# Six adaLN units computed in pairs, with their weights in an early pool and in idle buffers

## The chip, the cores and the metric

The kernel runs on one core of one Trainium2 chip. The metric is the device time of one execution in microseconds (us); lower is better.

## The reference

Two request groups go through one hybrid layer with the same weights: a prompt of 1024 frames and a sample of 32 frames. Everything is float32. Each group has its own conditioning vector `c`.

```python
mod = jax.nn.silu(c) @ w_ada + b_ada                 # 1024 -> 6 * 1024
sh1, sc1, g1, sh2, sc2, g2 = jnp.split(mod[:, None, :], 6, axis=-1)
h = x * (1 + sc1) + sh1
mq, mk, mv, mo, mi, mf, fq, fk, fv, ff, gu, gv = jnp.split(h @ w_in, split_at, axis=-1)
hm = mLSTM(mq, mk, mv, mo, mi, mf)                   # 4 heads, chunk-recurrent matrix memory
hf = forgetting_attention(fq, fk, fv, ff)            # 8 heads, causal softmax with a decay
hg = gu * spatial_gate(layer_norm(gv))               # gMLP
mix = jnp.concatenate([hm, hf, hg], -1) @ w_o
x = layer_norm(ALPHA * x + (1 + g1) * mix)
h = x * (1 + sc2) + sh2
y = (silu(h @ w_gate) * (h @ w_up)) @ w_down
x = layer_norm(ALPHA * x + (1 + g2) * y)
```

The first line, the adaLN product, is what the change touches. It is a product of a 1024 x 6144 matrix with two vectors, so nearly all of its cost lies in bringing 25 MB of weights to the core and in feeding TensorE a moving operand 256 columns wide for a result of two rows.

## The kernel before

**Numbers.** Every large product is done as three matmuls on float32 values split into a high and a low part (`hi*hi`, `hi*lo`, `lo*hi`), in three consecutive lines of the helpers (L130 to L132 in `gemm`, L402 to L404 in `tm_unit`).

**AdaLN units.** The 6144 columns are cut into 24 units of 256 columns; one unit is 1024 x 256 weights, 1 MB, loaded as two halves of 512 KB (`ada_load`). Units 0 to 7 hold shift and scale of the first modulation, 8 to 15 those of the second, 16 to 19 the gate `g1`, 20 to 23 the gate `g2`. `ada_parts(units, raws, ...)` computes one unit or a pair of units. For each half of each unit it makes four matmuls (L202); the trace shows each as two, so 16 rows a unit. They land in four strips of 32 partitions of one PSUM bank. ScalarE copies the bank to SBUF (L206, tile `adas`), TensorE transposes the two halves of the copy (L211, two instructions), VectorE sums the strips (L213) and adds the bias (`ada_end`, L219 and L223). One bank, one copy, one pair of transposes and one sum serve a whole group, be it one unit or two. The results go to the tile `mod`.

**Stages in order of time.** `fm_first` (to about 58 us) computes units 0 to 7 one by one between the first projection's products. Then two value units follow: `tm_unit(w1[0])` and `tm_unit(w1[1])`, each with one sample tile and eight tiles of 128 frames. A tile takes 24 matmuls of 264 columns, its PSUM bank is one of three (pool `pg`), and `evac_v` empties it: ScalarE copies the bank to `traw` (L434, two buffers), SyncE's queue stores `traw` to the output `o_v`, VectorE splits it into `vhl` (two buffers) and the queue stores that to the scratch tensor `dv`. Between tile 0 and tile 1 of the second value unit stands the pair of units 16 and 17 (`group`), whose four halves lie in the pool `pe`, tag `early`, with `EB` buffers. `tie` keeps the pair's matmuls behind the last matmul of the tile.

After that the constant `ORDER` is read word by word: `q` is a head's projection, `f` a head's attention for the first four blocks, `g` the next part of the gates (`gates`), `S` and `s` the decay of the sample and the start of the mLSTM states, `k` a key unit, `v`, `o` and `G` further projections, `m` an mLSTM chunk, and each `a` one adaLN unit from the list `rest` (`more(1)`). `T1[3]` units are taken ahead of the second part of the gates. So before the change the list is 18, 19, 8 to 15: units 18 and 19 are computed one by one at the gates, the others one at each of the eight `a`. All ten use the pool `pl`, tag `late`, with two buffers, which hold one unit. The pairs 20, 21 and 22, 23 come later, in the stage after the first layer norm.

**What sets the order.** The program is written in this order, but the tile framework's planner (`schedule_with_timeline_sim=True`) puts the instructions of each engine into a queue of its own. It takes an instruction when, by its reckoning, its inputs and its buffer are ready, and takes the one that was written first if several are. `high_priority(HPA)` moves `f` and `m` forward by 200. The queues are fixed when the program is built: on the chip each engine runs its queue in order, and waits at an instruction until its semaphores allow it. Nearly all loads and stores are in one queue, that of SyncE (SP). A pool opened in the space of a closed one can use a buffer only when the tiles that lay there are done with (`reuse_waits="tile"`).

**Buffers named by the change.** `mx` is at this point the pool `mx0`, opened when `pe` is closed. Its tags `mqk` (two buffers), `mb` and `mw` (one each) are used by the gates, by the decay of the sample and by every mLSTM chunk; `k1`, `k2`, `qp`, `q2` (two each) hold the operands of the heads in turn.

Of the kernel before, what the change touches and what calls it, by code (L numbers as in the profile page):

```python
# [7 lines left out]
F32 = mybir.dt.float32  # L8
F32R = mybir.dt.float32r
# [6 lines left out]
P = 128  # L16
D = 1024
KT = 8
S = 1024
# [13 lines left out]
LWE = 1  # L33
NB = (3, 2, 2)
PRE = 5
EB = 4
T1 = (0, 0, 0, 2)
XB, AB = (3, 6)
HPA = 200
MLB = (1, 2, 3, 4, 5)  # L40
RESE = "pp"
TAFF = ("aaaaaaaa", "aaaaaaav")
ORDER = "q0 f0 g q1 a f1 a g S q2 f2 k1p s a q3 f3 a v q4 f4 a q5 f5 o a m0 G0 q6 f6 a m1 G1p G2p q7 m2 f7 a m3 G3"
FP = (0, 0)
RAW = 3
WAKE = (10, 11)
# [19 lines left out]
def f(ap):  # L66
    return ap.bitcast(F32)


class Kernel:  # L70
# [115 lines left out]
    def ada_load(self, u, pool, tag, bufs):  # L186
# [3 lines left out]
            self.load(raws[half], self.d["w_ada"][u, :, half * 1024:(half + 1) * 1024])  # L190
        return raws

    def ada_parts(self, units, raws, ppool, ptag):
        self.phase = "ada"
        nc = self.nc
        n = len(units)
        ps = self.t(ppool, [P, 512], F32, ptag)
        steps = [(i, half) for half in ((0, 1) if units[0] < 8 else (1, 0)) for i in range(n)[::1 if half else -1]]
        for step in steps:
            i, half = step  # L200
            for k in range(4):
                nc.tensor.matmul(ps[32 * k:32 * k + 32, :256], self.c32[:, 4 * half + k, 6 - 2 * i:38 - 2 * i],  # L202
                                 raws[i][half][:, k * 256:(k + 1) * 256], start=step == steps[0],
                                 stop=step == steps[-1])
        a = self.t(self.pada, [P, 256], F32, "adas", 2)
        nc.scalar.copy(a, ps[:, :256])  # L206
        yield
        self.phase = "ada"
        pt = ps[:, 256:512]
        for half in range(2):  # L210
            nc.tensor.transpose(pt[:, half * P:(half + 1) * P], a[:, half * P:(half + 1) * P], self.ident)  # L211
        m = self.t(self.pada, [P, 2, 8], F32, "adam", 2)[:, :, :2 * n]
        nc.vector.tensor_reduce(m, pt.rearrange("p (h g j) -> p h j g", h=2, g=4)[:, :, 0:2 * n, :], AX.X, ALU.add)  # L213
        for i, u in enumerate(units):
            self.ada_end(u, m[:, :, 2 * i:2 * i + 2])
# [1283 lines left out]
    def run(self):  # L1499
        nc, tc, d = self.nc, self.tc, self.d  # L1500
        dr = self.pool("dr", space=DRAM)
        t = lambda shape, tag: self.t(dr, shape, F32, tag)
# [50 lines left out]
        sl = ExitStack()  # L1553
        self.pl = self.pada = self.pool("pl", ctx=sl)
        w1 = d["w_in_v"]
        rest = [18, 19] + list(range(8, 16))

        def more(n):
            for u in rest[:n]:
                self.ada((u,), self.pl, "late", 2, self.pt, "t")  # L1560
            del rest[:n]

        more(T1[0])
        se = ExitStack()
        pe = self.pool("pe", ctx=se, side="right")

        def group(units):
            def go():
                first = len(nc.cur_bb.bb.instructions)
                target = self.lastmm  # L1570
                for _ in self.ada_parts(units, raws, self.pt, "t"):
                    pass
                self.tie(nc.cur_bb.bb.instructions[first:], target, (mybir.EngineType.PE,))
                self.phase = "tm"
            raws = [self.ada_load(u, pe, "early", EB) for u in units]
            return go

        self.tm_unit(w1[0], 264, self.evac_v(0))
        self.tm_unit(w1[1], 264, self.evac_v(1), between={0: group((16, 17))})
        se.close()  # L1580
        s2 = ExitStack()
        self.mx = self.pool("mx0", ctx=s2)
        more(T1[2])
        gates = self.gates()
        next(gates)
        more(T1[3])
        self.foxbufs = (2, 2, 2, 2, 3)
        self.heads = {}

        def emit(x):  # L1590
            eng = nc.gpsimd if x[-1] == "p" else nc.vector
            x = x.rstrip("p")
            i = int(x[1:] or 0)
            if x[0] == "g":
                next(gates, None)
                return ()
            if x[0] == "f":
                return self.fox(i, ((0, 1, 2, 3),))
            if x[0] == "m":
                return self.mlstm(i)  # L1600
            if x[0] == "q":
                self.head_unit(i)
            elif x[0] == "k":
                self.fm_unit(w3[0], self.evac_mqk(3, 0.125), eng=eng)
            elif x[0] == "S":
                self.sample_decay()
            elif x[0] == "G":
                self.tm_unit(w2[2 + i % 2], 256, (self.evac_gv, self.evac_gmlp)[i % 2],
                             range(4 * (i // 2), 4 + i // 2 * 5), eng=eng)
            elif x[0] == "s":  # L1610
                self.mlstm_states()
            elif x[0] == "a":
                more(1)
            else:
                self.tm_unit(w2["vo".index(x)], 256, self.evac_raw((self.dmv, self.dmo)["vo".index(x)]), eng=eng)
            return ()

        for x in ORDER.split():
            if x[0] in "fm" and HPA:
                with tc.high_priority(HPA):  # L1620
                    weave(*[iter(emit(y)) for y in x.split("+")])
            else:
                weave(*[iter(emit(y)) for y in x.split("+")])
# [112 lines left out]
        t = self.t(self.pz, [P, 4, n], F32R, "z0", 1)  # L1736
# [129 lines left out]
```

## Time and profile before

| | |
|---|---|
| median of 3 runs | 1346.33 us (1344.91 to 1347.18) |
| profiled execution | 1346.69 us, span of its instructions 1344.9 us |
| TensorE (PE) busy | 1324.0 us, 98% |
| VectorE (DVE), ScalarE (ACT), GpSimd (POOL) busy | 989.1, 655.8, 231.9 us |
| granted TensorE clock | 0.998 |
| DMA | 221.73 MB, mean 165 GB/s |

How to read it: the span runs from the first to the last instruction; the execution's own time holds 1.8 us more. PE is the matmul stream, PEld the weight loads that overlap it; a busy PE is not one at its peak, since matmuls are pipelined and their ends are modelled. In a timeline a row gives the start, the length, the engine, the line, the operation, the tiles written and read, the number of merged instructions and, in brackets, the idle time before it with what ended it. `SPq` is SyncE's DMA queue: the row is the issue, not the transfer.

### The profile page before, as it was taken

The numbers are of one execution on the slowest core, as the hardware profiler recorded it, in microseconds if no ns is written. First come the engines' busy times: TensorE is split into PE (matmuls) and PEld (weight loads), VectorE is DVE, ScalarE is ACT, GpSimd is POOL, SyncE is SP. The second block draws the span as 40 slices with busy tenths as digits, with TensorE's granted clock in tenths as the row PEclk, the third lists the DMA queues.
The fourth block names the chain that finished last, engine by engine and source line by source line (L and its number), as shares of the span: only waits on it lengthen the run. The fifth ranks groups of instructions, "written<-read, shape, count | busy, mean of one in ns | idle before, by whom it ended". The sixth has DMA issues, their size and how long they took to land.

```text
span 1344.9 us, 25607 instructions
## 1 busy us (share of the span) xinstructions
PE 1324.0 (98%) x9684; PEld 1208.3 (90%) x9684; DVE 989.1 (74%) x2091; ACT 655.8 (49%) x1305; POOL 231.9 (17%) x263
## 2 busy tenths in 40 slices
PE   9999999999999999999999999999999999999996
PEld 6798888888999888888888888999999999999995
DVE  5635655678779667686876776678979887988777
ACT  3413445455547545545454454435754453635355
POOL 0102100143246100000000001464610000000341
PEclk9999999999999999999999999999999999999999
DMA  9585465546557754454344332663785858554221
GB/s 362 207 299 154 150 204 186 174 131 207 181 195 257 191 136 130 117 163 126 115 121 116 110 104 82 217 175 112 205 231 154 228 148 225 139 175 131 89 79 67
DMA packets 119450, 221.73 MB, mean 165 GB/s; under 512 B 18580, under 2 KB 62768, under 8 KB 119328
## 3 DMA queue, kind: packets, MB, share of 16 engines
q1 hardware_dynamic: 112096, 207.55, 49.0%
q0 software_dynamic: 6032, 11.94, 5.2%
q8 instruction: 76, 1.25, 0.4%
q10 hardware_dynamic: 1200, 0.62, 0.2%
q14 instruction: 46, 0.38, 0.1%
HBM read 188.13 MB, written 51.85 MB: 178 GB/s over the span
## 4 chain that ended last, share of the span: by engine, by line
PE 68%; DVE 4%; DMA 1%; ACT 1%; issue 1%; DVEq 0%; ACTq 0%
PE up_g L130 6%; PE up_g L132 6%; PE up_g L131 6%; PE dn_g L130 4%; PE dn_g L132 4%; PE dn_g L131 4%; PE sup_u L132 3%; PE sup_u L131 3%; PE sup_u L130 3%; PE wo_g L131 2%; PE wo_g L132 2%; PE wo_g L130 2%; PE sup_g L132 2%; PE sup_g L131 2%; PE sup_g L130 2%; PE fox_t L943 2%
## 5 line engine op out<-in xcount | busy, mean ns | idle before, releaser
L130 PE MATMUL up_g<-tm_ah,up_whi 128*128 128x512 f32 (+1 forms) x384 | 140.0, 365 | 0.0
L131 PE MATMUL up_g<-tm_al,up_whi 128*128 128x512 f32 (+1 forms) x384 | 140.0, 365 | 0.0
L132 PE MATMUL up_g<-tm_ah,up_wlo 128*128 128x512 f32 (+1 forms) x384 | 139.7, 364 | 0.0
L1368 ACT CAST sup_whi<-sup_raw 128x1024 fp32r<-128x1024 f32 x54 | 56.1, 1048 | 89.3 <-PE dn_u L131 43.9
L130 PEld LDWEIGHTS up_g<-tm_ah,up_whi 128*128 128x128 f32 x384 | 72.3, 188 | 11.1 <-DVE tm_al L1246 0.4
L132 PEld LDWEIGHTS up_g<-tm_ah,up_wlo 128*128 128x128 f32 x384 | 72.3, 188 | 11.1
L131 PEld LDWEIGHTS up_g<-tm_al,up_whi 128*128 128x128 f32 x384 | 72.3, 188 | 10.7
L916 ACT ACTIVATE fox_p<-fox_s,fox_fmx 128x384 f32<-128x384 f32 (+2 forms) x96 | 55.2, 579 | 53.0 <-DVE fox_fmx L914 41.2
L1199 DVE SCALAR_TENSOR_TENSOR wo_z<-dn_g,start_mod,wo_z 128x512 f32<-128x512 f32 (+4 forms) x120 | 60.3, 521 | 22.6 <-PE dn_g L132 22.0
L118 DVE TENSOR_TENSOR up_wlo<-up_raw,up_whi 128x1024 fp32r<-128x1024 f32 x50 | 65.2, 1305 | 15.0 <-ACT up_whi L117 13.7
L1369 DVE TENSOR_TENSOR sup_wlo<-sup_raw,sup_whi 128x1024 fp32r<-128x1024 f32 x54 | 68.0, 1263 | 10.7 <-ACT sup_whi L1368 10.7
L117 ACT CAST up_whi<-up_raw 128x1024 fp32r<-128x1024 f32 x50 | 52.4, 1048 | 47.2 <-PE up_g L131 23.9
L130 PE MATMUL dn_g<-up_acth,dn_whi 128*128 128x512 f32 (+2 forms) x200 | 73.5, 368 | 0.8 <-DVE wo_z L1199 0.8
L132 PE MATMUL dn_g<-up_acth,dn_wlo 128*128 128x512 f32 (+2 forms) x200 | 73.3, 366 | 0.0
L131 PE MATMUL dn_g<-up_actl,dn_whi 128*128 128x512 f32 (+2 forms) x200 | 72.8, 365 | 0.0
L948 ACT CAST fox_pth<-fox_t 128x512 fp32r<-128x512 f32 (+1 forms) x80 | 41.6, 542 | 59.2 <-PE fox_t L943 57.5
L117 ACT CAST dn_whi<-dn_raw 128x1024 fp32r<-128x1024 f32 (+1 forms) x44 | 42.7, 971 | 51.7 <-PE up_g L131 16.0
L911 DVE TENSOR_REDUCE fox_fmx<-fox_s 128x1 f32<-128x384 f32 (+2 forms) x96 | 52.8, 553 | 16.3 <-PE fox_s L908 15.0
L949 DVE TENSOR_TENSOR fox_ptl<-fox_t,fox_pth 128x512 fp32r<-128x512 f32 (+1 forms) x80 | 49.9, 631 | 15.9 <-ACT fox_pth L948 15.6
L118 DVE TENSOR_TENSOR dn_wlo<-dn_raw,dn_whi 128x1024 fp32r<-128x1024 f32 (+1 forms) x44 | 49.5, 1125 | 10.4 <-ACT dn_whi L117 9.5
L402 PE MATMUL tm_g<-tm_whi,start_h1h 128*128 128x256 f32 (+1 forms) x192 | 55.3, 288 | 0.7 <-DVE tm_traw L477 0.7
L1320 POOL DMA_DIRECT2D start_dp<-w_gu x19 | 19.8, 1067 | 209.0 <-DMA start_dp<-w_gu 209.0
(684 smaller groups left out, 4799.7 us busy)
## 6 DMA issues: line engine op xcount, KB each, us to landing
up_raw<-w_gu SPq DMA_DIRECT2D x50, 512.0 KB
ada_late<-w_ada SPq DMA_DIRECT2D x28, 512.0 KB
dn_raw<-w_dn SPq DMA_DIRECT2D x28, 512.0 KB
sup_raw<-w_gu SPq DMA_DIRECT2D x20, 512.0 KB
start_dp<-w_gu SPq DMA_DIRECT2D x19, 512.0 KB
start_dp<-w_gu POOLq DMA_DIRECT2D x19, 512.0 KB, 8.0
wo_raw<-w_o SPq DMA_DIRECT2D x18, 512.0 KB
sup_raw<-start_dp SPq DMA_DIRECT2D x18, 512.0 KB
```

What stands on the lines that cost most here:

```text
L117: nc.scalar.copy(hi[:, :w], raw[:, :w])
L118: (eng or nc.vector).tensor_tensor(lo[:, :w], raw[:, :w], f(hi[:, :w]), ALU.subtract)
L130: nc.tensor.matmul(ps, hi, xh(k), start=start and k == 0, stop=False)
L131: nc.tensor.matmul(ps, hi, xl(k), start=False, stop=False)
L132: self.lastmm = nc.tensor.matmul(ps, lo, xh(k), start=False, stop=stop and k == n - 1)
L402: nc.tensor.matmul(ps[:, :ncol], xh, hi, start=k == 0, stop=False)
L911: nc.vector.tensor_reduce(mxs[:, x:x + 1], s[:, :w], AX.X, ALU.max, negate=True)
L916: nc.scalar.activation(pr[:, lo:hi], banks[x][:, :hi - lo], AF.Exp, bias=mxs[:, 0:1], accum_out=sums[:, x:x + 1])
L949: nc.vector.tensor_tensor(pl[:, :e], ps[:, :e], f(ph[:, :e]), ALU.subtract)
L1199: self.lastz = self.nc.vector.scalar_tensor_tensor(z[:, m, x:y], ps[:, x - a:y - a], g[i], z[:, m, x:y], ALU.mult, ALU.add)
L1368: nc.scalar.copy(h, x)
L1369: tt(l, x, f(h), ALU.subtract)
```

## The change

Six of the ten single units become three pairs.

- Units 18 and 19 leave the list `rest`. They become a second `group` on the second value unit: their four halves are loaded into the pool `pe` (`EB` from 4 to 8), by loads written behind the pair 16, 17, and their matmuls stand behind tile 5. `T1[3]` becomes 0.
- Of the eight `a` in `ORDER` four stay (units 8, 9, 10 and 13). `A`, in the place of the one after `f3`, computes 11 and 12 as a pair; the `a` after `f4` is gone. `B`, in the place of the one after `f7`, computes 14 and 15; the `a` after `f6` is gone.
- The first unit of `A` and of `B` is loaded into the two `late` buffers as before. The second is loaded by the new `ada_spare` as four pieces of 512 columns: for `A` into one buffer of `mb`, one of `mw` and the two of `mqk`, for `B` into one buffer each of `k1`, `k2`, `qp` and `q2`.

```diff
-EB = 4
-T1 = (0, 0, 0, 2)
+EB = 8
+T1 = (0, 0, 0, 0)
...
-ORDER = "q0 f0 g q1 a f1 a g S q2 f2 k1p s a q3 f3 a v q4 f4 a q5 f5 o a m0 G0 q6 f6 a m1 G1p G2p q7 m2 f7 a m3 G3"
+ORDER = "q0 f0 g q1 a f1 a g S q2 f2 k1p s a q3 f3 A v q4 f4 q5 f5 o a m0 G0 q6 f6 m1 G1p G2p q7 m2 f7 B m3 G3"
...
+    def ada_spare(self, u, tags):
+        raws = []
+        for half in range(2):
+            tiles = [self.t(self.mx, [P, 512], dt, x, b) for x, dt, b in tags[2 * half:2 * half + 2]]
+            tiles = [f(x) if dt == F32R else x for x, (_, dt, _) in zip(tiles, tags[2 * half:2 * half + 2])]
+            for i, x in enumerate(tiles):
+                c = half * 1024 + i * 512
+                self.load(x, self.d["w_ada"][u, :, c:c + 512])
+            raws.append(tiles)
+        return raws
...
+                                 raws[i][half][k // 2][:, k % 2 * 256:k % 2 * 256 + 256]
+                                 if isinstance(raws[i][half], list) else
                                  raws[i][half][:, k * 256:(k + 1) * 256], start=step == steps[0],
...
-        rest = [18, 19] + list(range(8, 16))
+        rest = list(range(8, 16))
...
-        self.tm_unit(w1[1], 264, self.evac_v(1), between={0: group((16, 17))})
+        pairs = [group((16, 17))]
+        self.tm_unit(w1[1], 264, self.evac_v(1), between={
+            0: lambda: (pairs[0](), pairs.append(group((18, 19)))), 5: lambda: pairs[1]()})
...
+            elif x[0] in "AB":
+                tags = ((("mb", F32, 1), ("mw", F32, 1), ("mqk", F32, 2), ("mqk", F32, 2)) if x[0] == "A" else
+                        [(y, F32R, 2) for y in ("k1", "k2", "qp", "q2")])
+                raws = [self.ada_load(rest[0], self.pl, "late", 2), self.ada_spare(rest[1], tags)]
+                for _ in self.ada_parts(rest[:2], raws, self.pt, "t"):
+                    pass
+                del rest[:2]
```

The number of matmuls on weights, the bytes loaded and all results stay as they are.

## The prediction

> **What bounds the kernel now.** I read the page first, then the busy time by stage, the waits of TensorE, and the timelines of single queues at the places where the change cuts in.
>
> ```profile
> span 1344.9 us, 25607 instructions
> PE 1324.0 (98%) x9684; PEld 1208.3 (90%) x9684; DVE 989.1 (74%) x2091; ACT 655.8 (49%) x1305; POOL 231.9 (17%) x263
> ```
>
> TensorE works for 1324.0 of 1344.9 us. So a change gains by taking work off PE or by ending one of its few waits, and it loses by making PE wait. The waits of PE between the end of the first projection and the start of the output projection (57 to 460 us; columns: microseconds in total, times, longest) are few:
>
> ```profile
> PE fox_o L951 <- DVE fox_ptl L949: 1.1, 1, 1.1
> PE tm_g L416 <- DVE tm_traw L477: 1.0, 1, 1.0
> PE tm_g L416 <- ACT tm_traw L434: 0.7, 1, 0.7
> PE tm_g L402 <- DVE tm_traw L477: 0.7, 1, 0.7
> ```
>
> Three are among the heads, one (0.7, on `L434`) is between the two value units. That one matters most here, because it is the sign of another resource that is full. The stages by busy time (columns: length, PE, PEld, DVE, ACT, POOL, granted clock, DMA share, GB/s) show it:
>
> ```profile
> 62.00:82.00 20.00, 20.00 (x167) 20.00 (x166) 4.12 (x15) 1.90 (x5) 0.00 (x0) 1.00 1.01 346
> 82.00:86.00 4.00, 3.21 (x81) 2.83 (x81) 2.25 (x6) 2.79 (x6) 0.00 (x0) 1.00 0.54 199
> 110.00:210.00 100.00, 100.00 (x778) 87.59 (x778) 62.69 (x184) 48.51 (x113) 11.21 (x18) 1.00 0.58 177
> ```
>
> During the first value unit (62 to 82 us) the DMA engines are busy all the time, at 346 GB/s. PE has no gap there, but right behind it, in 82 to 86 us, it has lost 0.79 us. From 110 to 210 us the DMA has room (0.58) and PE has no gap at all. SyncE's queue and ScalarE's copies in that stretch tell why:
>
> ```profile
> 68.35 1.29 SPq L87 DMA_DIRECT2D tm_early<-w_ada  x2
> 70.93 0.34 SPq L91 DMA_DIRECT2D o_v<-tm_traw  x1
> 71.32 1.19 SPq L87 DMA_DIRECT2D tm_early<-w_ada  x2
> 72.62 0.51 SPq L91 DMA_DIRECT2D start_dv<-tm_vhl  x1
> 73.19 1.23 SPq L87 DMA_DIRECT2D ada_late<-w_ada  x2
> 74.76 0.37 SPq L91 DMA_DIRECT2D o_v<-tm_traw  x1
> ```
>
> ```profile
> 83.20 0.38 ACT L434 COPY tm_traw<-tm_g 128x264 f32<-128x264 f32 x1 [6.37 <-DMA o_v<-tm_traw]
> ...
> 84.46 0.38 ACT L434 COPY tm_traw<-tm_g 128x264 f32<-128x264 f32 x1
> ```
>
> ```profile
> 83.64 1.13 PE L416 MATMUL tm_g<-tm_raw,start_hs 128*32 128x66 f32 x64 [0.66 <-ACT tm_traw L434]
> ```
>
> Six halves of adaLN weights stand in the queue between the stores of the value tiles. The store of tile 3 is issued at 74.76, and the copy of tile 5, which needs its buffer, starts at 83.20 after 6.37 us of waiting. PE has three banks; they have carried it over all but 0.66 us of that. So this place has no slack left: whatever is put in front of these stores now is paid by PE.
>
> **Part 1: what pairing saves.** A pair costs less than two singles in two places. Rows of the pair 16, 17, of a single, and of a pair of transposes:
>
> ```profile
> 87.80 0.28 PE L404 MATMUL tm_g<-tm_whi,start_al 128*128 128x264 f32 x1
> 88.01 1.93 PE L202 MATMUL ada_t<-tm_early,start_c 128*32 128x256 f32 x32
> ...
> 90.11 0.29 PE L403 MATMUL tm_g<-tm_wlo,start_ah 128*128 128x264 f32 x1
> ```
>
> ```profile
> 131.23 0.29 PE L130 MATMUL fm_g<-start_h1h,gates_whi 128*128 128x272 f32 x1
> 131.45 1.07 PE L202 MATMUL ada_t<-ada_late,start_c 128*32 128x256 f32 x16
> ...
> 132.68 0.28 PE L132 MATMUL fm_g<-start_h1h,gates_wlo 128*128 128x272 f32 x1
> 132.81 0.29 PE L130 MATMUL fm_g<-start_h1h,gates_whi 128*128 128x272 f32 x1
> ```
>
> ```profile
> 135.33 0.29 PE L132 MATMUL fm_g<-start_h1h,gates_wlo 128*128 128x272 f32 x1
> 135.46 0.38 PE L211 MATMUL ada_t<-start_ident,ada_adas 128*128 128x128 f32 x2
> 135.59 0.38 PE L130 MATMUL fm_g<-start_h1h,gates_whi 128*128 128x272 f32 x1
> 135.80 0.28 PE L131 MATMUL fm_g<-start_h1l,gates_whi 128*128 128x272 f32 x1
> ```
>
> I count from start to start, since the lengths overlap. An ordinary step takes 132.81 - 132.68 = 0.13. The pair takes 90.11 - 87.80 = 2.31 less two ordinary steps, 2.05. The single takes 132.68 - 131.23 = 1.45 less two steps, 1.19; two make 2.38. So a pair saves 0.33 in matmuls: one entry and one exit, not a matmul fewer. The transposes cost 135.80 - 135.33 = 0.47 less two steps, 0.21, and each pair does without one set. That is 0.54 us a pair, 1.6 us for three, all on PE, which has no gaps in this stretch. This is the whole direct gain: 0.12%.
>
> In the Trainium skill, "TensorE: Matmul & The Clock Gate", section "Part 4: PE-mode transpose", a transpose is put at about 275 ns in a kernel's context; six of them would be 1.65 us instead of 0.6, and the gain 2.6 us. The trace gives 270 to 272 ns as the length of one too, but starts the next matmul 0.13 us after, so I keep 0.21 for two.
>
> Three copies on ACT and three sums on DVE go too; both have idle time (49% and 74% busy), so I set them at nothing, and they would count only where PE waits for these engines, as in the two waits on `L477`.
>
> **Part 2: what moves.** The loads of 18 and 19 were the first two users of the `late` buffers. Unit 18's are the two rows at 73.19, though its call stands behind the whole second value unit: the planner issues a load as soon as its buffer is open. After the change 16 to 19 have eight open buffers at once, and the two `late` buffers are open too, now for unit 8. Hence I expect ten halves in the queue where there were six: the four of 16, 17, the four of 18, 19 directly behind, two of unit 8. The four more are 4 x 0.524 = 2.1 MB. At the 346 GB/s of the window they take 6.1 us, ahead of the stores of tiles 3 to 5.
>
> PE is already waiting there, so the delay reaches it almost whole. I take off 0.6 us: the copy of tile 6 came 1.26 us behind that of tile 5 (83.20 to 84.46) because ACT takes them one by one, and about half of that can absorb a later store. The stall: 5.5 us, beside the 0.66 that exist. Its bounds: nothing, if all four are issued behind the stores; 2.4, if only two of them are ahead (half of 6.1 less 0.6); 7, if the four move at the 305 GB/s of the slowest part of that window.
>
> ```profile
> 70.00:74.00 4.00, 4.00 (x35) 4.00 (x34) 1.65 (x6) 0.76 (x2) 0.00 (x0) 1.00 1.04 305
> ```
>
> It is not given back: after 110 us the DMA has room, but there PE is what the kernel waits for.
>
> Nothing is won where the load of 19 and the matmuls of both leave (130 to 146 us), beyond part 1: PE has 100.00 of 100.00 us there. Closing `pe` five tiles later, each of 24 ordinary steps, opens the heads' and gates' buffers some 15 us later. The first in the queue that want them are these loads, which would come at about 105 us. What uses them, the first heads' attention and the gates, stands behind the second value unit's last tile, so I set this at nothing.
>
> ```profile
> 90.39 1.45 SPq L87 DMA_DIRECT2D head_v<-start_dv  x2
> ```
>
> `A` and `B` each add two issues (four quarters of 256 KB for two halves), and the bytes stay. `mb` and `mw` are free only when the sample's decay is stored, at 191.72; the mLSTM now loads `mb` at 193.78. So the first chunk comes behind `A`'s matmuls. It cannot end early anyway: its output gate is loaded at 232.53. I set this at nothing, with -1 to +1.5 us for the order of the heads that changes: one wait of the size 1.1 less or more.
>
> ```profile
> 191.72 0.29 SPq L91 DMA_DIRECT2D start_dsf<-foxd_mb  x1
> ...
> 193.78 0.34 SPq L87 DMA_DIRECT2D mlstm_mb<-start_dM  x1
> ...
> 232.53 0.34 SPq L87 DMA_DIRECT2D mlstm_mo<-start_dmo  x1
> ```
>
> **The sum.** -1.6 + 5.5 = +3.9 us. The span goes from 1344.9 to 1348.8; the profiled execution (1346.69) would be 1350.6, and the median of the runs, 0.36 lower, 1350.2. Its own range: stalls of 2.4 to 7 and -1 to +1.5 for the order of the heads, 1346 to 1353.
>
> **Rivals.**
>
> *The loads wait their turn.* If the planner puts the four halves behind the stores of the first value unit, they run in the free DMA time later on and the change is worth its 1.6 us: 1344.7. For it: the loads are written behind tile 0 of the second unit, and the stores come first in the program. Against it: unit 18's loads were written later still and went ahead. The Trainium skill has this rival as a rule ("DMA: Bandwidth & Descriptors", section "Rules for kernel authors"): issue a DMA early and wait late, so that its cost overlaps. By that rule four earlier loads cost nothing; the trace speaks against it here, with 6.37 us of waiting behind earlier loads.
>
> *Faster.* The loads cost nothing and the new order also ends the three waits among the heads, 1.1 + 1.0 + 0.7 = 2.8: 1346.3 - 1.6 - 2.8 = 1341.9. Nothing in the trace ties these waits to the adaLN units; two are waits for DVE.
>
> *The first chunk stops the heads.* `A` holds all buffers of the mLSTM, its work bunches behind `A`, and PE twice waits for a softmax chain as it does now once, 2 x 1.1 us on top of the forecast: 1352.4. It decides if `A`'s matmuls come after 232.5 us, when the first chunk could end otherwise. Against it: the unit after `f3` has its place between two heads' attention and a projection, long before the output projection `o` that makes the gate.
>
> **How the numbers follow.** A measurement of this kernel can tell about 0.2%, 2.7 us, from no change. Forecast 0.64, of which 0.56 lie above +2.7 and 0.08 (small stalls) within; the loads in turn 0.20, of which 0.18 within and 0.02 below -2.7; the faster case 0.11; the stopped heads 0.05. Faster 0.13, same 0.26, slower 0.61. The range goes from 1343.8, which takes in the case of loads in turn, to 1353.0, the top of the forecast; it leaves out the faster case and most of the last.
>
> **What would show it.** Right: ten adaLN halves issued between 68 and 82 us, DMA share at 1.0 until about 88 us, the copies of tiles 6 and 7 some 6 us later, a wait of PE on `L434` of 5 to 6 us behind the first value unit, 36 transposes in place of these 42:
>
> ```profile
> L211 PE MATMUL ada_t<-start_ident,ada_adas x42: 270/272/332, 8.0 to 441.7; 128*128 128x128 f32 x42
> ```
>
> Wrong: `early` loads issued after 84 us, no wait of PE above 1 us before 110 us, or a gain or loss that lies after 190 us.

## The result, and the profile after

The changed kernel takes 1348.76 us (median of 22 runs, 1346.17 to 1351.78); 22 runs of the kernel before beside it have a median of 1345.38. The ratio is 1.0025, 95% interval 1.0018 to 1.0031: 3.4 us slower, 2.4 to 4.2. The profiled execution took 1348.93 us.

The head of the page after shows nearly the same TensorE work (before: 1324.0 us and 9684 matmul rows, six transposes more), in a longer span:

```profile
span 1347.2 us, 25587 instructions
...
PE 1324.5 (98%) x9678; PEld 1210.4 (90%) x9678; DVE 992.5 (74%) x2088; ACT 655.6 (49%) x1302; POOL 231.1 (17%) x263
```

Waits of PE in the same stretch as in the prediction, 57 to 460 us (total, times, longest; lines from about 200 on have moved by 11 to 13, so `L447` is the former `L434`):

```profile
PE tm_g L429 <- ACT tm_traw L447: 3.0, 1, 3.0
PE tm_g L415 <- DVE tm_traw L490: 1.8, 1, 1.8
PE wo_g L130 <- DVE wo_z L1212: 1.6, 3, 1.2
PE tm_g L415 <- ACT tm_tmsum L433: 1.0, 1, 1.0
PE tm_g L415 <- DVE tm_brt L477: 0.6, 1, 0.6
```

The wait between the value units has grown from 0.7 to 3.0. A wait on `wo_z` in the output projection is new; the prediction had nothing there.

SyncE's queue, ScalarE's copies and PE at the place the prediction spoke of:

```profile
70.70 0.82 SPq L87 DMA_DIRECT2D tm_early<-w_ada  x2
71.60 0.39 SPq L91 DMA_DIRECT2D o_v<-tm_traw  x1
72.03 1.29 SPq L87 DMA_DIRECT2D tm_early<-w_ada  x2
73.43 0.61 SPq L91 DMA_DIRECT2D start_dv<-tm_vhl  x1
74.10 1.09 SPq L87 DMA_DIRECT2D tm_early<-w_ada  x2
75.46 0.61 SPq L91 DMA_DIRECT2D o_v<-tm_traw  x1
76.75 0.33 SPq L87 DMA_DIRECT2D tm_early<-w_ada  x1
77.17 0.82 SPq L91 DMA_DIRECT2D start_dv<-tm_vhl  x1
79.88 0.33 SPq L87 DMA_DIRECT2D tm_early<-w_ada  x1
81.11 1.00 SPq L87 DMA_DIRECT2D ada_late<-w_ada  x2
83.08 0.34 SPq L91 DMA_DIRECT2D o_v<-tm_traw  x1
```

```profile
85.89 0.38 ACT L447 COPY tm_traw<-tm_g 128x264 f32<-128x264 f32 x1 [8.31 <-DMA o_v<-tm_traw]
91.91 0.38 ACT L447 COPY tm_traw<-tm_g 128x264 f32<-128x264 f32 x1 [2.68 <-DMA o_v<-tm_traw]
92.84 0.38 ACT L447 COPY tm_traw<-tm_g 128x264 f32<-128x264 f32 x1 [0.55 <-DVE tm_vhl L453]
```

```profile
83.04 0.29 PE L417 MATMUL tm_g<-tm_whi,start_h1l 128*128 128x264 f32 x1
86.32 1.99 PE L429 MATMUL tm_g<-tm_raw,start_hs 128*32 128x66 f32 x64 [3.00 <-ACT tm_traw L447]
```

Ten halves are issued between 70.7 and 82 us. The `o_v` store at 75.46 stands behind six of them, as the one at 74.76 did before. The next stands behind all ten, and so goes out at 83.08. The copies on ScalarE follow the stores: the three shown, of tiles 5, 6 and 7, were at 83.20, 84.46 and 85.68 before, and are at 85.89, 91.91 and 92.84. PE stands still for 3.0 us, until 86.3. The 64 small matmuls behind the gap then take 1.99 us instead of 1.13. The windows tell why (columns as before: length, PE, PEld, DVE, ACT, POOL, granted clock, DMA share, GB/s):

```profile
82.00:86.00 4.00, 1.32 (x11) 1.10 (x10) 0.50 (x2) 0.11 (x1) 0.00 (x0) 0.95 1.03 408
...
86.00:88.00 2.00, 1.68 (x64) 1.68 (x64) 0.90 (x2) 2.00 (x3) 0.00 (x0) 0.50 1.02 419
88.00:90.00 2.00, 1.02 (x15) 0.78 (x8) 2.00 (x4) 1.01 (x5) 0.00 (x0) 0.50 1.02 389
90.00:92.00 2.00, 2.00 (x11) 2.00 (x11) 0.47 (x3) 0.09 (x1) 0.00 (x0) 0.50 0.97 351
92.00:94.00 2.00, 2.00 (x18) 1.82 (x20) 1.02 (x4) 0.67 (x2) 0.00 (x0) 0.90 0.91 321
```

TensorE has half its clock until about 92.4 us. The Trainium skill describes such a gate ("TensorE: Matmul & The Clock Gate", section "HAM oscillation — how this bites in real kernels"): there a kernel is to have no gap of PE over about 3.4 us, or the clock falls to half. Here the clock fell with a gap of 3.0 us.

**Where the span's 2.3 us lie.** I split both profiles at the first matmul that writes a tile, up to the last matmul of all, and take the difference of each stretch. The value units run from the last `fm_t` to the first `head_g`, the heads to the first `wo_g`, the output projection to the first `up_g`. By the prediction's rows, the pair 18, 19 brings 2.26 (2.05 + 0.21) into the first stretch, and the heads lose two singles (2.80) and two pairings (1.08). "Net" is what is left when this is taken off.

| stretch | after less before | of it moved or saved work | net |
|---|---|---|---|
| start and first projection | +0.33 | 0 | +0.33 |
| value units | +7.78 | +2.26 | +5.52 |
| heads | -5.98 | -3.88 | -2.10 |
| output projection | +2.08 | 0 | +2.08 |
| 991 to 1018 us | -1.68 | 0 | -1.68 |
| all the rest | -0.04 | 0 | -0.04 |
| in all, to the last matmul | +2.49 | -1.62 | +4.11 |

In this profile the value units lost the forecast 5.5, but as 2.3 more of the first wait (3.0 for 0.7), 1.0 of a second (`tm_tmsum`) and the rest, about 2.2, as half clock. How much of that the loads made is taken up behind the table of all profiles. The stretch at 991 to 1018 us is a hiccup of the one profile of before, where PE waited for these two. Every other kernel below has 1.4 to 1.7 us less there, also the one with unused loads, in which every engine's order is that of before from 106 us on. So the two profiles lie 1.7 us too close together.

```profile
PE dn_g L130 <- DVE wo_z L1199: 0.8, 1, 0.8
PE dn_u L130 <- DVE wo_z L1199: 0.4, 1, 0.4
```

### The profile page after: what moved, and what is told of

Read it like the earlier page. It is cut to its first block, busy times and chain, and to the rows that moved or that the text cites. A ratio compares the mean times of both kernels' runs of the same rounds, so it can differ in the third digit from the quotient of the medians.

```text
span 1347.2 us, 25587 instructions
## 1 busy us (share of the span) xinstructions
PE 1324.5 (98%) x9678; PEld 1210.4 (90%) x9678; DVE 992.5 (74%) x2088; ACT 655.6 (49%) x1302; POOL 231.1 (17%) x263
## 4 chain that ended last, share of the span: by engine, by line
PE 69%; DVE 3%; DMA 2%; issue 1%; ACT 1%; SPq 0%; POOL 0%; DVEq 0%; POOLq 0%; ACTq 0%
PE up_g L132 6%; PE up_g L130 6%; PE up_g L131 6%; PE dn_g L130 4%; PE dn_g L132 4%; PE dn_g L131 4%; PE sup_u L132 3%; PE sup_u L131 3%; PE sup_u L130 3%; PE sup_g L131 2%; PE sup_g L132 2%; PE sup_g L130 2%; PE wo_g L130 2%; PE wo_g L132 2%; PE wo_g L131 2%; PE fox_t L956 2%
## 5 line engine op out<-in xcount | busy, mean ns | idle before, releaser
L415 PE MATMUL tm_g<-tm_whi,start_ah 128*128 128x256 f32 (+1 forms) x192 | 55.9, 292 | 1.5 <-ACT tm_tmsum L433 1.0
```

The lines of the kernel that those rows point to most:

```text
L415: nc.tensor.matmul(ps[:, :ncol], xh, hi, start=k == 0, stop=False)
```

## The experiments

Two theories stood against each other. *Queue*: four early loads ahead of the value stores are the whole loss. *Heads*: the loss comes from the pairs `A` and `B` and the order that they bring. Every ratio is to runs of the kernel before on the same chip, and the microseconds are worked out from it. The difference of the medians is another by up to 0.4; where it is more, both are given.

**The pair 18, 19 alone** (`ORDER` of before):

```diff
-ORDER = "... q3 f3 A v q4 f4 q5 ... q6 f6 m1 ... m2 f7 B m3 G3"
+ORDER = "... q3 f3 a v q4 f4 a q5 ... q6 f6 a m1 ... m2 f7 a m3 G3"
```

> Only the pair 18, 19 on the second value unit; units 8 to 15 stay single at their eight places. Theory 'queue' (the four early halves of 18, 19 stand ahead of the stores of the value tiles, PE waits there and its clock falls): +5.5 for the wait and the clock, -0.5 for one pair, so about +5 us, 1350.4, with the wait of PE on L434 and the granted clock of 0.82 in 86 to 104 us as in the changed kernel. Rival 'heads' (the loss is made by A and B, their buffers and the new order of the heads): -0.5 us, 1344.9, no change before 110 us.

Measured: 1348.55, ratio 1.0019 (1.0008 to 1.0031), +2.5 us. Slower, but half of what "queue" asked. The wait on `L447` was 0.9, a second one on `tm_tmsum` 1.5, and the clock stayed at 1.00 there, where 0.82 was expected.

**`A` and `B` alone** (the loads and matmuls of 18 and 19 as before):

```diff
-EB = 8
-T1 = (0, 0, 0, 0)
+EB = 4
+T1 = (0, 0, 0, 2)
...
-        rest = list(range(8, 16))
+        rest = [18, 19] + list(range(8, 16))
...
-            0: lambda: (pairs[0](), pairs.append(group((18, 19)))), 5: lambda: pairs[1]()})
+            0: lambda: pairs[0]()})
```

> Only A and B; 18 and 19 stay single at the gates, four early buffers as before. Theory 'queue': two pairs save 2 x 0.54, so -1.1 us, 1344.3, and 62 to 104 us look as in the kernel before (wait of 0.7 us on L434, clock 1.00). Rival 'heads': most of the +3.4 us of the change, 1348 or more, with new waits after 190 us.

Measured: 1348.41, ratio 1.0022 (1.0011 to 1.0033), +2.9 us, where "queue" expected a gain. So neither theory is the whole.

**Loads moved behind the stores**, all else as changed (`issue_after` holds them until the last store of the first value unit is issued):

```diff
-            raws = [self.ada_load(u, pe, "early", EB) for u in units]
+            with tc.issue_after(behind[0]) if units[0] == 18 else ExitStack():
+                raws = [self.ada_load(u, pe, "early", EB) for u in units]
...
+        behind = [i for i in nc.cur_bb.bb.instructions if i.engine == mybir.EngineType.SP][-1:]
```

> The changed kernel with one difference: the four halves of 18, 19 are queued behind the last store of the first value unit. Theory 'queue': the wait on L434 is back at 0.7 us, the clock stays at 1.00, and what is left is the saving of three pairs, -1.6 us, 1343.8; at worst the loads, needed after tile 5 at about 104 us, hold the pair up by 1 us. Rival 'heads': no better than the changed kernel, 1348.8.

Measured: 1346.92, ratio 1.0007 (0.9995 to 1.0019), +0.9 us. 2.5 of the 3.4 us are gone by moving four DMA issues; the two intervals hardly overlap (the changed kernel's begins at 1.0018). The wait on `L447` was 0.7 and the clock 1.00 between the value units, as expected. It is no faster than before, as "queue" wanted it to be.

**The wait filled**, to see whether the half clock is a cost of its own:

```diff
+        first, target = len(nc.cur_bb.bb.instructions), self.lastmm
+        fill = self.t(self.pss, [P, 512], F32, "s")
+        for _ in range(20):
+            nc.tensor.matmul(fill[:, :P], self.onesm, self.onesm, start=True, stop=True)
+        self.tie(nc.cur_bb.bb.instructions[first:], target, (mybir.EngineType.PE,))
```

> The changed kernel with 20 products of a constant 128x128 tile, whose result is not used, put into PE's queue between the two value units, where PE now waits 3.0 us; by the rows of the start they take 0.12 us each, 2.4 us. If the fall of the clock comes from the idle time and is a cost of its own: the wait falls to about 0.6 us, the granted clock stays near 1.00 in 86 to 104 us, and about 2.2 us come back: +1.2 against the kernel before, 1346.6. If the wait for the stores is all: the wait is filled, nothing is won, +3.4, 1348.8.

Measured: 1352.84, ratio 1.0049 (1.0034 to 1.0065), +6.6 us, 3.2 more than the changed kernel (by the medians 4.1 more). The clock stayed at 1.00 from 62 to 110 us, but the experiment does not settle the question, because the filling was too long. Each of the 20 products is two rows of the trace, and together they took 4.63 us where 2.4 were meant:

```profile
82.79 4.63 PE L1596 MATMUL tm_s<-start_onesm 128*128 128x128 f32 x40
87.35 1.13 PE L429 MATMUL tm_g<-tm_raw,start_hs 128*32 128x66 f32 x64
91.03 0.39 PE L415 MATMUL tm_g<-tm_whi,start_ah 128*128 128x264 f32 x1 [2.56 <-ACT tm_traw L447]
```

The copy for which PE had waited there was done at 85.1, so the filling itself held PE for some 2 us, and at the next tile PE waited 2.6 us for a copy behind a late store. The profile also lost 3.4 us near 977 us, with half clock for 3.4 us after waits of 1.3 and 0.8. Whether the half clock is a cost of its own stays open.

**The loads without the pairing.** Before, with the four halves loaded a second time, read by nothing:

```diff
-EB = 4
+EB = 8
...
+            0: lambda: (pair(), [self.ada_load(u, pe, "early", EB) for u in (18, 19)])})
```

> The kernel before with eight `early` buffers and the four halves of units 18 and 19 loaded into them a second time, directly behind 16 and 17; nothing reads them, and 18 and 19 stay single units at the gates. All matmuls and ORDER are those of before; only 2.1 MB more stand in the queue. Theory 'queue' (the loads ahead of the stores are the whole of the value part): 2.5 us measured for the value pair alone plus the 0.54 that its pairing saves, so about +3.0 over before, 1348.4, with the wait on ScalarE's copy between the value units at 2 us or more. Rival 'planner' (what costs is the new order of instructions that any change of the program brings, wherever it is): +0 to +1, 1345.4 to 1346.4, since the matmuls are the same.

Measured: 1349.97, ratio 1.0033 (1.0020 to 1.0045), +4.4 us. All matmuls are those of before and only DMAs are added, so the loads cost time without any pairing. In the traces TensorE's 9684 and GpSimd's 263 instructions stand in the same order as before; in the other queues the order differs between 73 and 106 us only, where ScalarE now takes the copies of tiles 6 and 7 behind its next casts. Its windows beside the prediction's (3.21 of 4 us and a DMA share of 0.54 before):

```profile
82.00:86.00 4.00, 2.26 (x74) 1.88 (x72) 0.73 (x2) 1.95 (x3) 0.00 (x0) 1.00 1.03 411
86.00:104.00 18.00, 16.84 (x153) 15.77 (x154) 8.43 (x34) 3.73 (x12) 0.00 (x0) 1.00 0.88 317
```

PE loses 0.95 and 1.16 us, in waits of 1.4 (`L434`, 0.7 before) and 1.5 (`tm_tmsum`), while the DMA engines are full until 92 us (1.02 to 1.05 in every 2 us); the clock stays at 1.00. This profile lost 2.1 us here, less than its median did.

**`A` alone and `B` alone**:

```diff
A_only:
-ORDER = "... m0 G0 q6 f6 m1 G1p G2p q7 m2 f7 B m3 G3"
+ORDER = "... m0 G0 q6 f6 a m1 G1p G2p q7 m2 f7 a m3 G3"
B_only:
-ORDER = "... s a q3 f3 A v q4 f4 q5 f5 o a m0 ..."
+ORDER = "... s a q3 f3 a v q4 f4 a q5 f5 o a m0 ..."
```

> The kernel before with the pair A alone (units in the mLSTM's buffers); 18 and 19 and the two last units stay single. Heads' pairs together measured +2.9. Theory 'borrowed mLSTM buffers': A carries it, +2.9 plus 0.5 or so, 1348.3 to 1348.9, with a wait of PE among the mLSTM chunks or at wo_z. Rival 'B is late': A saves its 0.54, 1344.9.

> The kernel before with the pair B alone (units in buffers of the seventh head). Theory 'borrowed mLSTM buffers': B saves its 0.54, 1344.9, and the wait of PE on wo_z in the output projection is gone. Rival 'B is late': B carries the 2.9 through a new wait on wo_z right behind it, 1348.3 to 1348.9.

Measured: `A` 1347.36, ratio 1.0011 (1.0001 to 1.0021), +1.5 us; `B` 1348.55, ratio 1.0018 (1.0009 to 1.0028), +2.4 us. `B` brings the wait in the output projection, with 2.0 us on `wo_z`; `A` has none there, and loses on single waits among the heads (`mlstm_s` on a DMA 1.6, `fox_s` on a softmax 1.4) that some profiles with `A` have and others don't.

Why `B` does it can be read from three queues. Before, VectorE, then GpSimd:

```profile
371.62 0.50 DVE L492 SCALAR_TENSOR_TENSOR fm_qkl<-fm_g,start_qsc,fm_qkh 128x272 fp32r<-128x272 f32 x1 [1.69 <-DMA start_dql<-fm_qkl]
372.03 0.48 DVE L1199 SCALAR_TENSOR_TENSOR wo_z<-wo_g,start_mod,wo_z 128x256 f32<-128x256 f32 x1
```

```profile
372.20 0.77 POOL L496 TENSOR_TENSOR fm_qkr<-fm_qkh,fm_qkl 128x272 f32<-128x272 f32 x1 [3.40 <-DVE fm_qkl L492]
...
376.25 7.58 POOL L1193 TENSOR_TENSOR wo_z<-wo_z,wo_pv 128x256 f32<-128x256 f32 x7 [2.22 <-ACT wo_pv L1057]
```

After, VectorE, GpSimd, and PE:

```profile
372.09 0.48 DVE L1212 SCALAR_TENSOR_TENSOR wo_z<-wo_g,start_mod,wo_z 128x256 f32<-128x256 f32 x1
...
376.50 0.49 DVE L505 SCALAR_TENSOR_TENSOR fm_qkl<-fm_g,start_qsc,fm_qkh 128x272 fp32r<-128x272 f32 x1
...
381.06 3.88 DVE L1084 TENSOR_TENSOR wo_zs<-wo_z 128x256 f32<-128x256 f32 x1
```

```profile
377.13 1.62 POOL L509 TENSOR_TENSOR fm_qkr<-fm_qkh,fm_qkl 128x272 f32<-128x272 f32 x1 [5.21 <-DVE fm_qkl L505]
...
379.76 4.89 POOL L1206 TENSOR_TENSOR wo_z<-wo_z,wo_pv 128x256 f32<-128x256 f32 x7
```

```profile
385.49 0.36 PE L130 MATMUL wo_g<-tm_ah,wo_whi 128*128 128x256 f32 x1 [1.24 <-DVE wo_z L1212]
```

The last key projection's `fm_qkl` now stands behind the first `wo_z` in VectorE's queue and comes 4.9 us later, though the stage began only 2.1 us later. GpSimd's `fm_qkr` waits for it, with the seven `wo_z` subtractions queued behind. They start at 379.76 instead of 376.25, and VectorE's first sum `wo_zs` beside them takes 3.88 us where it took 0.45 before, seemingly waiting for them; what it waits for was not told apart. The next evacuation of a PSUM bank is late, and PE waits. No adaLN instruction is near: `B`'s matmuls ran at 350 us, its transposes at 354.

**The value pair with late loads, without `A` and `B`** (the two edits above together):

> The pair 18, 19 on the second value unit with its four loads behind the last store of the first value unit, and ORDER of before (neither A nor B). Theory 'queue': only the pairing's 0.54 is left, 1344.9, the wait between the value units is back at 0.7 to 1 and nothing new at wo_z. If new waits come with any change of order ('planner'): 1346.5 to 1347.5.

Measured: 1346.52, ratio 1.0005 (0.9993 to 1.0016), +0.7 us. With the loads ahead it was +2.5. Nothing new at `wo_z`, as expected. But the wait between the value units was 2.3, where 0.7 to 1 was expected, with no load ahead of the stores (below).

**`B` behind `f6` instead of `f7`**, where VectorE's and GpSimd's queues keep the order of before at this place; on the kernel before, then on the changed one:

```diff
-... q6 f6 m1 G1p G2p q7 m2 f7 B m3 G3"
+... q6 f6 B m1 G1p G2p q7 m2 f7 m3 G3"
```

> The kernel before with the pair B alone, but written behind f6 instead of f7 (14 and 15 are then taken before m1). In the kernels with B behind f7, VectorE's queue has the last key projection's fm_qkl behind the first wo_z and GpSimd's queue has its fm_qkr ahead of the seven wo_z subtractions; with B behind f6 both stand as in the kernel before. Theory 'queue order' (that swap is what B costs): the wait of PE on wo_z is gone, the 2.4 of B behind f7 too, and the pairing's 0.54 is left, 1345.0 to 1346. Rival 'buffers of a head' (B is dear because its quarters take a head's buffers, wherever it stands): +2 or more, 1347.8 to 1349.

> The changed kernel with B behind f6 instead of f7, the early loads of 18 and 19 as they are. Theory 'queue order': 2.4 less than the changed kernel's 1348.8, so 1346.4, with the wait on ScalarE's copy between the value units as large as in the changed kernel. Rival 'buffers of a head' or 'the loads are all of it': no change, 1348.8.

Measured: alone 1347.33, ratio 1.0014 (1.0003 to 1.0024), +1.9 us; in the changed kernel 1348.77, ratio 1.0014 (1.0003 to 1.0026), +1.9 us (by the medians +3.1). The wait on `wo_z` is gone in both, so the swapped order did make it. But the time is not back: the first lies 1.3 above the range of "queue order" and just short of the rival's +2, and the median of the second is the rival's 1348.8. That `B` costs through the buffers of a head, wherever it stands, is not excluded. PE waits in the same stage for other things instead (`B` behind `f6` alone):

```profile
PE wo_g L130 <- ACT tm_ah L1144: 0.8, 1, 0.8
PE ada_t L213 <- DMA ada_late<-w_ada: 0.7, 1, 0.7
...
PE wo_g L131 <- DVE tm_al L1145: 0.5, 2, 0.3
```

**The loads behind, once more, and both mended** (loads behind the stores, and `B` behind `f6`):

> The changed kernel with the loads of 18 and 19 behind the last store of value unit one, looked at once more for its profile: waits at wo_z about 2 us, between the value units about 1 us.

> The changed kernel with both faults mended: the loads of 18 and 19 behind the last store of value unit one, and B behind f6. All three pairs stay. Theory 'queue' plus 'queue order': only the pairing is left, -1.6, 1343.8; with the 1 us that A and the late loads were seen to cost, 1344.8. It would be the only one of these kernels that is not slower than before. Rival: 1346.9 as with the loads alone.

Measured: the first, a single execution, 1343.85, with 1.7 at `wo_z` and 1.3 between the value units. Both mended: 1348.48, ratio 1.0017 (1.0007 to 1.0028), +2.3 us (by the medians +2.8), slower than either theory asked: the repair failed. Its profile has a wait of 2.9 on `L447` and 3.4 us of half clock behind it, with the loads behind the stores. No kernel tried was faster than the one before.

**The profiles in one table**, net as above, in us against the profile of before (without the filled wait, whose filling lies in the value units; its output projection lost 3.0):

| kernel | value units | heads | output projection |
|---|---|---|---|
| loads ahead: changed kernel | 5.5 | -2.1 | 2.1 |
| loads ahead: value pair alone | 1.7 | 1.9 | -0.2 |
| loads ahead: unused | 2.1 | 1.1 | 0.0 |
| loads ahead: `B` behind `f6` | 1.1 | -0.7 | 1.9 |
| loads behind: changed kernel | 0.7 | 2.5 | 2.5 |
| loads behind: the same, once more | 0.6 | -2.1 | 2.1 |
| loads behind: value pair alone | 1.6 | 0.3 | 0.2 |
| loads behind: `B` behind `f6` | 3.7 | -0.8 | 1.7 |
| no early loads: `A` | -0.1 | 2.4 | 0.0 |
| no early loads: `B` | 2.6 | 1.0 | 2.4 |
| no early loads: `A` and `B` | 1.1 | 0.3 | 2.2 |
| no early loads: `B` behind `f6` | -0.8 | 0.4 | 2.9 |

The output projection is clear: every profile with `B`, wherever it stands, loses 1.7 to 3.0 there, every one without it -0.2 to 0.2. The heads are not: one and the same kernel lost 2.5 and won 2.1, the 2.5 and the value pair's 1.9 each hold 3.4 us of half clock, which by half of it are worth up to 1.7, and the kernel with the unused loads lost 1.1 there with every queue as before.

The value units lie between: 2.6 on average with the loads ahead, 1.7 behind, 0.7 without, with a spread of 3 to 4.5 us in each group. Much of that is chance. With `B` alone every engine's queue is that of before up to 258 us, and this profile still lost 2.6 there. Nor does the wait on `L447` follow the loads: 3.0, 1.4, 0.9 and 0.3 with them ahead, 2.9, 2.3, 1.3 and 0.7 with them behind. What does follow them is the next copy. With the loads ahead, the copy of tile 6 comes 5.9 to 7.3 us behind that of tile 5, in all five profiles. In the nine others it comes 1.2 to 2.4 us behind, as here with the value pair and the loads behind:

```profile
85.07 0.38 ACT L447 COPY tm_traw<-tm_g 128x264 f32<-128x264 f32 x1 [8.09 <-DMA o_v<-tm_traw]
...
86.33 0.37 ACT L447 COPY tm_traw<-tm_g 128x264 f32<-128x264 f32 x1
```

What PE pays for that late copy is harder to name: at the tile behind the wait on `L447` it waits 1.0 to 1.5 for `tm_tmsum` in the four profiles of the table with the loads ahead, 0.8 to 1.3 for `tm_traw` in three others, and not at all in the rest.

For the size the times of the runs decide: loads alone +4.4; with them behind the stores, 2.5 less in the changed kernel and 1.8 less with the value pair. With `B` behind `f6` it is not seen (1.9 ahead, 2.3 behind; by the medians 3.1 and 2.8).

## Why the prediction was right

The forecast was 1350.2 and slower by +3.9; measured was 1348.8 and +3.4. The sign and one of the mechanisms held, the late stores. The agreement in size is in part luck: two errors cancel, a stall taken too large and a cost in the output projection left out.

- *Three pairs save 1.6.* 36 transposes stand where 42 were, as said, and the matmuls of the pair 18, 19 take 2.30 (from 110.51 to 112.81), by the count that gave 2.31 for 16, 17. No run shows the 1.6 as a gain, since each pair came with more than it saved.

```profile
L224 PE MATMUL ada_t<-start_ident,ada_adas x36: 270/272/332, 8.2 to 445.9; 128*128 128x128 f32 x36
```

- *Ten halves ahead of the stores; copies late; PE waits on `L434`.* Right but for the last step: halves at 70.7 to 82, DMA share over 1.0 until 90, the copies of tiles 6 and 7 7.5 and 7.2 us later (about 6 was said), and loads alone cost time. Six halves stood ahead of the store at 74.76 already, and the four new ones came in front of the store after it. So the wait on `L434` belongs to the earlier store, and the profiles do not show that the loads make it longer; what they make late is the copy of the next tile.
- *The stall is 5.5.* The profile lost 5.52 there, but as a wait of 3.0, not of 5 to 6, and the rest at the next tile and as half clock, which the prediction did not have. That it came to 5.5 is luck: this was the dearest of the four profiles with the loads ahead, which lost 2.6 on average, and waits of 2.3 and 2.9 at this place came with the loads behind, too. By the runs the loads cost 1.8 to 4.4 us, but for the pair of kernels with `B` behind `f6`. So the term was too large: it took PE to pay the whole transfer time of four halves, less 0.6. (The 1.26 us between two copies, from which the 0.6 was taken, is not copying: a cast of 1.08 us stands between them.)
- *The order of the heads at nothing, -1 to +1.5.* This step failed. `A` and `B` alone cost 2.9 (1.5 to 4.4) where a gain of 1.1 was due, so the term is about +4 for that kernel; 2.1 of it is the output projection, in every kernel with `B`. The prediction followed the moved instructions to their buffers and to the first mLSTM chunk, and stopped there. It asked who waits for what was moved, and not which other instructions the planner would deal out in another order. One of the signs that it gave for being wrong, "a gain or loss that lies after 190 us", did come.
- *Rivals.* Loads in turn: refuted by the queue above, and bringing them into turn did not give 1344.7 but 1346.9. The rule of the Trainium skill that was cited with it ("DMA: Bandwidth & Descriptors", section "Rules for kernel authors") speaks of the fixed setup cost; four loads that nothing waits for cost 4.4 here. Faster: of the three waits among the heads, the 1.1 on `fox_ptl` was gone in the changed profile and the two on `tm_traw` were 1.8 instead of 1.7; the stretch as a whole gained 2.1, but not reliably. First chunk: no sign of it in the changed kernel; a wait of `mlstm_s` for a load (1.6 and 1.4) came in two profiles with `A` and stayed away in the others.

By the parts: -1.6 for pairing, +1.8 to 4.4 for the loads and about +2.1 for the output projection make +2.3 to +4.9, around the 3.4 measured. What stays open is why `B` brings waits into the output projection even where the queue order at `wo_z` is that of before, what makes `A` cost 1.5 (0.1 to 2.8), and why the kernel with both faults mended is still 2.3 slower. That the parts do not add up (2.5 and 2.9 alone, 3.4 together) is just within the intervals.

## What to carry to other kernels

Four loads of half a megabyte, issued early into free buffers, are not free if stores that release buffers stand behind them in the same queue and the DMA engines are full: look at who is queued behind before asking who needs the data. Where a planner orders the queues, even a pair of instructions less changes the order of stages that it never touches, so cost such an edit by a range taken from the waits that other orders of the same kernel show, not at nothing. And a gain of 0.5 us for a pair is smaller than what moving it can cost: no place where the pairs were put showed a gain. A last one: a stretch of one profile that matches the forecast is no proof, as long as the same instructions in the same order can differ by half of it from one profile to the next.

## What was not expected of the hardware

With a gap of 3.0 us TensorE ran at half clock for about 6.8 us, by the rows above (6.0 from 86 to 92, and 0.4 in each of the windows with 0.90 beside them). One of 2.9 us brought 3.4 us of half clock (both faults mended). In other profiles gaps of 2.3 (value pair, loads behind), 2.4 (`A` and `B` alone) and 2.6 us (filled wait) left the clock at 1.00, but among the heads single waits of 1.9 (changed kernel, loads behind) and 1.6 us (`B` alone) were followed by 3.4 us of it. With `B` alone it also came after waits of 0.7 and 1.2 us, with 64 small matmuls between them (columns as above):

```profile
86.00:88.00 2.00, 1.52 (x8) 1.53 (x9) 2.00 (x5) 1.93 (x6) 0.00 (x0) 0.72 0.38 144
88.00:90.00 2.00, 2.00 (x11) 2.00 (x10) 2.00 (x7) 0.39 (x2) 0.00 (x0) 0.50 0.82 125
90.00:92.00 2.00, 2.00 (x25) 1.52 (x27) 0.51 (x5) 0.38 (x1) 0.00 (x0) 0.93 0.96 371
```

Yet longer pairs of waits around the same 64 matmuls, 1.4 and 1.5 with the unused loads and 0.9 and 1.5 with the value pair alone, left the clock at 1.00. So in these profiles the length of a wait does not decide whether the clock falls, and what does is not shown. Each time it fell before the last stage, half clock lasted 3.4 us, in the changed kernel twice that. The Trainium skill's 3.4 us (the section named above) speaks of a single gap; here shorter ones were followed by half clock, and the measurement decides.
